# One strip of modulation columns computed behind the last down product of the first feed-forward

## The chip, the cores and the metric

The kernel runs on one core of a Trainium2 chip. The metric is the time of one execution in device microseconds (us). TensorE (PE) multiplies matrices; VectorE (DVE), ScalarE (ACT) and GpSimd (POOL) do the element-wise work; SyncE (SP) issues nearly all loads. Each engine runs its own instructions in order and waits on semaphores for the others. Transfers are issued by SP, ACT and POOL and carried out by the DMA engines.

## The reference

One inference step of a decoder layer for 512 new prompt tokens (one sequence) and 64 sample tokens (eight sequences of eight), 576 token columns in all, with model width 1024. A vector of 9 x 1024 modulation columns per sequence is computed from a conditioning vector by one matrix, and its nine parts shift, scale and gate the three sub-layers:

```
m = jax.nn.silu(c) @ w_ada + b_ada
sh1, sc1, g1, sh2, sc2, g2, sh3, sc3, g3 = jnp.split(m[:, None, :], N_MOD, axis=-1)
h = modulate(rms_norm(x, n1_g), sh1, sc1)
x = x + 0.5 * g1 * swiglu(h, w1_gate, w1_up, w1_down)
h = modulate(rms_norm(x, nm_g), sh2, sc2)
mix, S_new, v_rows = token_mix(h, pos0, S0, w_in, ...)
x = x + g2 * mix
```

A second feed-forward with sh3, sc3, g3 follows. The modulation matrix `w_ada` is 1024 x 9216 in f32, so it is 36 MB of weights that must all be read.

## The kernel before

The kernel keeps the activations transposed, with 128 channels on the partitions and the 576 tokens as columns, and multiplies with f32 weights split into a high and a low part (three matmuls for each product). A weight block is loaded into a raw buffer (`wraw`), ACT casts its high part, DVE subtracts to get the low part, and PE multiplies.

**Strips.** The modulation columns are made in strips of 512 of the 9216 columns. Strips 0 to 3 are made first in another cut. Strips 4 to 17 are made by `ada_strip` (L335): for each half `kk` of the 1024 rows it loads two tiles of 512 KB into the pool `ada` (two buffers), then runs four products with `ada_mm` (L305), each of which fills 32 of the 128 output rows of one PSUM bank. ACT copies the bank (`ada_copy`, L313), PE transposes it in four pieces (`ada_turn`, L319), and `ada_add` sums four groups and adds the bias (DVE, L324 and L328). Strip 10 holds the first half of g2, which is used only after the token mixer.

**Where strips run.** They are generators that `tick` advances by an estimated time, so their instructions fall between the products of the big loops. Strips 4 to 9 run in the first feed-forward. Strips 10 to 17 are started with `start(ada_rest(range(10, 18), 7.0), 9.0)` (L1276) and run in the loop of pairs of w_in columns behind it, called the stream of pairs below (`stream(pair2(w))`).

**Between the two.** The last down product of the first feed-forward is `last_down1`. It has an order written out by hand, `INTO_MIX`; `run` issues the steps in that order and ties each engine except SP to it. The steps named in this text:

- `Dch` is the product for channel block c and token part h; `rsch` adds it to the residual x on DVE (L466); `spch` spills x to DRAM by an ACT-issued transfer (`x1d`, L1223); `sqch`, `adch` form the sum of squares (ACT L428; POOL or DVE L433).
- `rdh`, `rqh`, `qih` turn the sum into 1/rms for half h: a PE product with ones (L444), an ACT reciprocal square root (L448), three DVE steps (L456 to L461). `xph` multiplies x by it (DVE L533); `bpc` and `sp` modulate (ACT L540, DVE L549).
- `N11`, `B21`, `N1`, `B22` and the like, with `h` or `l` and a number, split the modulated blocks into high (ACT L564, L566) and low parts (DVE L571, L575) for PE.
- `h0a0`, `h0a1`, `h0b0` and so on are the products of the first two pairs of w_in columns (L651), and `sn0`, `sn1` copies of their banks (ACT L660). `P1`, `P2`, `P5`, `P6` belong to the third pair.
- `Whc`, `Wlc` split the down weights; those of c = 6 and 7 live in the pool `xs1`, which has three buffers of 9 KB a partition.

SP has no written order; its loads go out in the order in which the scheduler places them, each once its buffer is free.

Of the kernel before, what the change touches and what calls it, by code (L numbers as in the profile page):

```python
# [8 lines left out]
F32 = mybir.dt.float32  # L9
# [6 lines left out]
P = 128  # L16
# [37 lines left out]
INTO_MIX = """  # L54
D00 D01 rs00 Wh2 sp00 sq00 ad00 Wl2 D10 rs01 px0 Wh3 sq01 ad01 Wl3 D11 sp01 rs10 sp10 sq10
ad10 Wh6 D20 rs11 Wl6 px1 sq11 sp11 ad11 D21 Wh4 rs20 sq20 Wl4 sp20 ad20 D30 rs21 Wh5 px2
sq21 Wl5 sp21 ad21 D40 rs30 sq30 sp30 ad30 Wh7 Wl7 D50 rs40 sq40 sp40 nh0 ad40 D60 rs50
sq50 nl0 sp50 ad50 wh0 D70 rs60 sq60 sp60 wl0 ad60 D31 rs70 sq70 nh1 sp70 ad70 nl1 D41 rs31
px3 sq31 sp31 rd0 wh1 D51 ad31 rq0 rs41 px4 q00 sq41 wl1 q10 sp41 ad41 q20 D61 rs51 px5 x00 sq51
sp51 ad51 D71 x10 b000 b010 x20 b100 x30 b110 N11h0 rs71 N11h1 rs61 px7 b210 N11l0 px6  # L60
sq71 N11l1 sq61 sp61 sp71 b300 ad61 h0a0 b310 b200 ad71 B21h3 B21h2 B21l3 B21l2 rd1 sn0 h0a1
rq1 q01 q11 q21 x01 h0b0 x11 b01 b00 s0 b11 s1 b10 tx0 sn1 tx1 N1h0 x21 h0b1 N1h1 N1l0 N1l1
b20 x31 b21 T2a1 b31 b30 h1a0 s3 e0s1 s2 B22h3 N3c1 B22h2 T2b1 N3h1 B22l2 p2bh T2h1 B22l3
h1a1 p2ah p2bl T2l1 e0s0 e0m0 p2al e0m1 N3l1 h1b0 p2S N4c1 p2U N4h1 T2a0 p2Sh P1 e1t0 T2b0
e1m0 p2Sl T2h0 h1b1 e1a0 T2l0 e1s0 P1s p2V N3c0 p2Uh P2 N4c0 N3h0 p2Ul N4h0 P5 e1a1 N3l0
# [19 lines left out]
def layer_kernel(ctx: ExitStack, tc: tile.TileContext, a):  # L85
    nc = tc.nc
    PE, DVE, ACT, POOL = nc.tensor, nc.vector, nc.scalar, nc.gpsimd
# [28 lines left out]
    turn = [0, 0]  # L116
# [17 lines left out]
    def nine(home, shape, dt=F32R):  # L134
        return now[home].tile(shape, dt, tag="x", name=nm(home), bufs=4 if home == "xa" else 3)
# [9 lines left out]
    def bank():  # L145
        return pp.tile([P, 512], F32, tag="ps", name=nm("ps"), bufs=8)
# [51 lines left out]
    def run(order, steps):  # L198

        traced = nc.cur_bb.bb.instructions  # L200
        first = traced[-1]
        for s in order.split():
            steps.pop(s)()
        assert not steps, steps
        at = next(k for k in reversed(range(len(traced))) if traced[k] is first)
        last = {}
        for i in traced[at + 1:]:
            if i.engine != mybir.EngineType.SP:
                if i.engine in last:
# [39 lines left out]
    vec = lines(cst, [P, 104], name="vec")  # L249
# [15 lines left out]
    def ada_tile(shape=(P, 2, 512)):  # L265
        return adas.tile(list(shape), F32, tag="ada", name=nm("ada"), bufs=2)
# [13 lines left out]
    mT = lines(cst, [P, 72, 9], name="mT")  # L280
# [9 lines left out]
    for i in range(2):  # L290
        for n in range(NT):
            rows = P if n < 4 else NS
            t = first.tile([rows, 512], F32, name=nm("xt"))
# [11 lines left out]
    def ada_mm(ps, k, w):  # L305
        g = k % 4
        PE.matmul(
            ps[32 * g:32 * g + 32], lhsT=cs[:, k, :], rhs=w, start=k < 4, stop=k >= 4, tile_position=(0, 32 * g)
        )

    def ada_copy(ps):
        M = now["M"]()
        ACT.copy(out=M, in_=ps)  # L313
        return M

    def ada_turn(M):
        p2 = bank()
        for j in range(4):
            PE.transpose(p2[:, j * P:(j + 1) * P], in_=M[:, j * P:(j + 1) * P], identity=ident)  # L319
        return p2  # L320

    def ada_add(p2, dst, bias):
        t = tp.tile([P, 4, 9], F32, tag="m", name=nm("m"), bufs=2)
        DVE.tensor_reduce(  # L324
            out=t, in_=p2.rearrange("p (j g x) -> p j x g", j=4, g=4)[:, :, 0:9, :],
            axis=mybir.AxisListType.X, op=ALU.add,
        )
        DVE.tensor_tensor(out=dst, in0=t if len(dst.shape) == 3 else t.rearrange("p (m j) c -> p m j c", m=2),  # L328
                          in1=bias, op=ALU.add)
# [25 lines left out]
    class First:  # L355

        def __init__(self, p):
            self.p, self.ws = p, []
            for k in range(KC):
                if k % 4 == 0:  # L360
                    e = nine("xa" if p < 2 or (p, k) == (3, 4) else "xs1", [P, 4, 512], F32)
                w = e[:, k % 4]
                nc.sync.dma_start(
                    out=w.rearrange("p (m c) -> p m c", m=2),
                    in_=a["w_ada"][0, k * P:(k + 1) * P, :].rearrange("p (m c) -> p m c", m=9)[
                        :, 0:2, p * 256:(p + 1) * 256],
                )
# [571 lines left out]
    class Down:  # L939
# [151 lines left out]
    steps = {**operand_steps(Late()), **pair_steps(pairs, greg)}  # L1091
    for c in range(KC):
# [11 lines left out]
        out=xall[:, :, NP:T], in_=psS[:, 0:KC * NS].rearrange("p (c t) -> p c t", c=KC))  # L1104
# [88 lines left out]
    def last_down1(W, product):  # L1193
        finish(rest)
        gate, g, ps, rest_of = gate1m(), a2(), {}, {}
        warm(AF.Abs_reciprocal_sqrt)
        ops.clear()
        ops["near"] = ("B22", "N3", "N4")
        O = Operands(g, 3)
        steps = {}  # L1200
        for c in (2, 3, 6, 4, 5, 7):
            W.load(c)
            steps[f"Wh{c}"] = lambda c=c: W.hi(c)
            steps[f"Wl{c}"] = lambda c=c: W.lo(c)
        w = rg(0), rg(1)
        p = {i: Plain2(w[i][0], i, w[i][1].out, w[i][1].post) for i in range(2)}
        pairs[3] = p[2] = pair2(qk(0))
        steps.update(operand_steps(O))
        ends = pair_steps(p, None)
        for n in ("Gh0", "Gl0", "Gh1", "Gl1"):  # L1210
            ends.pop(n)
        steps.update(ends)
        for c, h in LAST:
            def d(c=c, h=h):
                ps[c, h] = product(c, h)

            def rs(c=c, h=h):
                rest_of[c] = resid(xs[c], ps[c, h], c, h, gate)

            steps[f"D{c}{h}"], steps[f"rs{c}{h}"] = d, rs  # L1220
            steps[f"sq{c}{h}"] = lambda c=c, h=h: n2.square(xs[c], h)
            steps[f"ad{c}{h}"] = lambda h=h: n2.sum(h)
            steps[f"sp{c}{h}"] = lambda c=c, h=h: nc.scalar.dma_start(out=x1d[:, c, HALF[h]], in_=xs[c][:, HALF[h]])  # L1223
            if h:
                steps[f"px{c}"] = lambda c=c: rest_of[c]()
        for h in range(2):
            norm_steps(steps, n2, O, h)

# [44 lines left out]
            yield 6.0  # L1273

    start(operands_of_values(), 4.0)
    start(ada_rest(range(10, 18), 7.0), 9.0)  # L1276
    for w in (
        [qk(hd) for hd in range(1, HEADS)] + [rg(hd) for hd in range(2, HEADS)]
        + [gb(c) for c in range(0, KC, 2)] + [ga(c) for c in range(0, KC, 2)]
# [548 lines left out]
    for pr in ([0], [1], [2], [3], [4], [5], [6, 7]):  # L1828
# [52 lines left out]
    steps = {**operand_steps(O), **pair_steps(pairs, greg)}  # L1881
# [173 lines left out]
```

## Time and profile before

| | before |
|---|---|
| time, median of 3 runs | 1652.28 us (1651.71 to 1655.64) |
| the profiled execution | 1651.52 us |
| its span in the trace | 1649.7 us |
| granted TensorE clock, mean | 0.996 |
| DVE busy | 1152.9 us (70%) |
| ACT busy | 783.2 us (47%) |
| DMA | 252.09 MB, mean 153 GB/s |

The span runs from the first to the last instruction; the profiled execution took 1.82 us more than its span. Busy times are shares of the span. Rows of a timeline give the start in us, the busy time, the engine, the source line, the operation, the tile written and the tiles read, the shapes, the count of merged instructions, and in brackets the idle time of the engine before the row with what ended it.

### The profile page before, as it was taken

Reading aid. Unit: us, or ns where it says so; the run is one execution under the profiler, and the core shown is the slowest. Engines: PE = TensorE matmul, PEld = TensorE weight load, DVE = VectorE, ACT = ScalarE, POOL = GpSimd, SP = SyncE. Lnnn points to the kernel's source line nnn. Section 1 sums busy time; section 2 is a strip of 40 time slices with the busy share of each in tenths; the row PEclk is TensorE's granted clock in tenths of the full one; section 3 lists DMA queues with packets and bytes.
Section 4 is the critical chain, followed back from the end, with each engine's and each line's share of the span. In section 5 each row is a group of like instructions: output and inputs, shape, how many; then the busy total and the mean of one; then the engine's idle time right before and its main releaser. Section 6 shows DMA issues by size and latency. Waiting matters only on the chain. (4 is left out here: it accounts for less than half of the span.)

```text
span 1649.7 us, 31367 instructions
## 1 busy us (share of the span) xinstructions
PE 1618.0 (98%) x12548; PEld 1554.7 (94%) x12548; DVE 1152.9 (70%) x1835; ACT 783.2 (47%) x1331; POOL 292.0 (18%) x372
## 2 busy tenths in 40 slices
PE   7999999999999999999999999999999999999997
PEld 4899999999999999999999999998999999999997
DVE  6867856676697777854788554676848868676773
ACT  5644524344564556553444454443236525343454
POOL 0000000000411111113346343454231000000002
PEclk9999999999999999999999999999999999999999
DMA  9553444332536776765467575799540333332331
GB/s 292 152 157 110 141 129 139 110 110 84 183 115 212 228 214 192 222 196 187 126 192 248 180 172 159 208 261 270 177 141 14 87 93 97 91 96 80 100 90 58
DMA packets 300212, 252.09 MB, mean 153 GB/s; under 512 B 13593, under 2 KB 260633, under 8 KB 300066
## 3 DMA queue, kind: packets, MB, share of 16 engines
q1 hardware_dynamic: 284594, 206.76, 41.5%
q0 software_dynamic: 13168, 40.97, 8.8%
q10 hardware_dynamic: 2304, 2.36, 0.4%
q8 instruction: 98, 1.61, 0.4%
q14 instruction: 48, 0.39, 0.1%
HBM read 207.01 MB, written 43.02 MB: 152 GB/s over the span
## 5 line engine op out<-in xcount | busy, mean ns | idle before, releaser
L651 PE MATMUL ps<-xa,whl 128*128 128x288 f32 x3000 | 420.6, 295 | 5.8 <-ACT xa L564 2.4
L651 PEld LDWEIGHTS ps<-xa,whl 128*128 128x128 f32 x3000 | 401.7, 189 | 18.5 <-issue 5.0
L651 PE MATMUL ps<-xs,whl 128*128 128x288 f32 x2040 | 287.2, 294 | 1.3 <-ACT sn L660 1.1
L651 PEld LDWEIGHTS ps<-xs,whl 128*128 128x128 f32 x2040 | 272.2, 188 | 11.6 <-ACT sn L660 4.6
L679 DVE TENSOR_TENSOR whl<-wraw,whl 128x1024 fp32r<-128x1024 f32 x192 | 234.5, 1223 | 54.0 <-ACT whl L669 45.1
L669 ACT CAST whl<-wraw 128x1024 fp32r<-128x1024 f32 x192 | 200.2, 1048 | 107.0 <-DVE wraw L793 67.3
L485 PEld LDWEIGHTS ps<-c,wd 128*128 128x128 f32 x1824 | 236.7, 188 | 3.5 <-issue 3.4
L485 PE MATMUL ps<-c,wd 128*128 128x320 f32 (+1 forms) x1824 | 239.9, 292 | 0.0
L485 PE MATMUL ps<-c,whl 128*128 128x256 f32 (+1 forms) x1368 | 186.9, 294 | 1.1 <-ACT c L195 0.7
L485 PEld LDWEIGHTS ps<-c,whl 128*128 128x128 f32 x1368 | 179.4, 188 | 3.4 <-ACT c L195 1.2
L472 POOL TENSOR_TENSOR x<-x,s 128x64 f32<-128x64 f32 x72 | 35.2, 489 | 796.9 <-DVE s L471 771.0
L466 DVE SCALAR_TENSOR_TENSOR x<-ps,gate,x 128x320 f32<-128x320 f32 (+1 forms) x128 | 61.1, 481 | 110.7 <-PE ps L485 110.7
L660 ACT COPY sn<-ps 128x288 f32<-128x288 f32 x195 | 77.2, 398 | 104.0 <-PE ps L651 103.7
L188 DVE TENSOR_TENSOR whl<-wraw,whl 128x1024 fp32r<-128x1024 f32 x56 | 76.3, 1364 | 66.7 <-ACT whl L187 66.1
L952 ACT CAST wd<-wraw 128x640 fp32r<-128x640 f32 (+2 forms) x58 | 45.4, 783 | 102.6 <-PE ps L485 95.5
L1353 PE MATMUL ps<-whl,xx 128*128 128x256 f32 x768 | 88.9, 276 | 0.0
L1353 PEld LDWEIGHTS ps<-whl,xx 128*128 128x128 f32 x768 | 88.0, 188 | 0.0
L651 PE MATMUL ps<-xs,whs 128*128 128x288 f32 x480 | 69.1, 292 | 0.0
L187 ACT CAST whl<-wraw 128x1024 fp32r<-128x1024 f32 x56 | 58.6, 1049 | 21.5 <-PE ps L485 13.3
L669 ACT CAST whs<-wraw 128x512 fp32r<-128x512 f32 x62 | 38.4, 620 | 55.7 <-PE ps L651 45.0
L651 PEld LDWEIGHTS ps<-xs,whs 128*128 128x128 f32 x480 | 64.8, 188 | 0.0
L957 DVE TENSOR_TENSOR wd<-wraw,wd 128x640 fp32r<-128x640 f32 (+2 forms) x58 | 53.5, 922 | 10.6 <-ACT wd L952 10.5
(285 smaller groups left out, 2219.0 us busy)
## 6 DMA issues: line engine op xcount, KB each, us to landing
ada<-in_w_ada_dram SPq DMA_DIRECT2D x56, 512.0 KB
wraw<-in_w_in_dram SPq DMA_DIRECT2D x96, 256.0 KB
wraw<-in_w_gate_dram SPq DMA_DIRECT2D x88, 256.0 KB
wraw<-in_w_up_dram SPq DMA_DIRECT2D x88, 256.0 KB
wraw<-in_w_in_dram SPq DMA_DIRECT2D x32, 512.0 KB
wraw<-in_w_down_dram SPq DMA_DIRECT2D x32, 384.0 KB
wraw<-in_w_down_dram SPq DMA_DIRECT2D x32, 320.0 KB
accd<-c POOLq DMA_DIRECT2D x32, 288.0 KB, 5.9
```

The costliest lines, as they stand in the source:

```text
L187: ACT.copy(out=hi, in_=raw)
L188: now["lo"] = (eng or DVE).tensor_tensor(out=lo, in0=raw, in1=hi.bitcast(F32), op=ALU.subtract)
L466: DVE.scalar_tensor_tensor(out=x[:, o:o + w], in0=ps[:, :w], scalar=g[:, c, 0:1], in1=x[:, o:o + w], op0=ALU.mult, op1=ALU.add)
L472: return lambda: POOL.tensor_tensor(out=x[:, NP:T], in0=x[:, NP:T], in1=u, op=ALU.add)
L485: PE.matmul(ps[:, :PW[h]], lhsT=s[:, k, c0:c0 + P], rhs=m[:, PART[h]], start=k == 0 and z == 0, stop=k == kc - 1 and z == 2,)
L651: PE.matmul(ps[:, :H], lhsT=s[:, j * P:(j + 1) * P], rhs=m[:, j, :], start=fresh and j == 0 and z == 0, stop=j == 3 and z == 2, skip_group ...
L660: ACT.copy(out=t, in_=ps[:, :H])
L669: ACT.copy(out=hl[:, 0], in_=src)
L679: now["lo"] = DVE.tensor_tensor(out=hl[:, 1], in0=src, in1=hl[:, 0].bitcast(F32), op=ALU.subtract)
L952: ACT.copy(out=hl[:, 0], in_=self.raw[c])
L957: DVE.tensor_tensor(out=lo, in0=self.raw[c], in1=hi.bitcast(F32), op=ALU.subtract)
L1353: PE.matmul(ps[:, :DV], lhsT=s, rhs=m, start=i == 0, stop=i == 23)
```

## The change

Strip 10 leaves the generators and gets a class `Strip` whose steps stand in `INTO_MIX`:

- Its first two tiles (`load(0)`, in the pool `ada`) are asked for in `last_down1` before the second pair's loads. The other two are halves of one buffer of `xs1` and are asked for by the step `Ad`, behind `Wh7`.
- `A0` and `A1`, eight products in all, stand behind `D71`, the last down product.
- `Ac`, the ACT copy of the bank, stands behind `sn0` and overwrites a part of the first weight tile. `At`, the four transposes, stands behind `rq1`. `Aa`, the reduce and the add on DVE, stands behind `N1l1`.
- The generators start with strip 11.

```diff
-sp51 ad51 D71 x10 b000 b010 x20 b100 x30 b110 N11h0 rs71 N11h1 rs61 px7 b210 N11l0 px6
+sp51 ad51 D71 A0 A1 x10 b000 b010 x20 b100 x30 b110 N11h0 rs71 N11h1 rs61 px7 b210 N11l0 px6
...
+    class Strip:
+        def load(self, kk, w):
+            self.w[kk] = w
+            for i, t in enumerate(w):
+                k0 = 4 * kk + 2 * i
+                nc.sync.dma_start(
+                    out=t,
+                    in_=a["w_ada"][0, k0 * P:(k0 + 2) * P, self.s * 512:(self.s + 1) * 512].rearrange(
+                        "(k p) c -> p k c", p=P),
+                )
+        def mm(self, kk):
+            if kk == 0:
+                self.ps = bank()
+            for g in range(4):
+                ada_mm(self.ps, 4 * kk + g, self.w[kk][g // 2][:, g % 2, :])
+        def copy(self):
+            self.M = self.w[0][0][:, 0]
+            ACT.copy(out=self.M, in_=self.ps)
...
+        strip = Strip(10)
+        strip.load(0, [ada_tile() for _ in range(2)])
...
+        def near():
+            e = nine("xs1", [P, 4, 512], F32)
+            strip.load(1, [e[:, 2 * i:2 * i + 2] for i in range(2)])
+        steps["Ad"], steps["Ac"], steps["At"], steps["Aa"] = near, strip.copy, strip.turn, strip.add
+        for kk in range(2):
+            steps[f"A{kk}"] = lambda kk=kk: strip.mm(kk)
...
-    start(ada_rest(range(10, 18), 7.0), 9.0)
+    start(ada_rest(range(11, 18), 7.0), 9.0)
```

**On PE**, from the end of the last down product (`xw_`, step D71) to the products of the first two pairs. Before:

```order
L485 MATMUL ps_4939<-c_4491,xw_4737 128x256
L651 MATMUL ps_4987<-xa_4965,whl_4763 128x288 x12
L651 MATMUL ps_4988<-xa_4965,whl_4763 128x288 x12
L444 MATMUL ps_5021<-all_4587,onesr 128x288
L651 MATMUL ps_5027<-xa_4965,whl_4840 128x288 x12
L651 MATMUL ps_5028<-xa_4965,whl_4840 128x288 x12
L651 MATMUL ps_4987<-xa_5016,whl_4791 128x288 x12
```

And now, in the changed kernel, where L651 has become L684 and L444 has become L477:

```order
L518 MATMUL ps_4946<-c_4491,xw_4741 128x256
L307 MATMUL ps_4965<-ada_4565,cs 32x512 x2
L307 MATMUL ps_4965<-ada_4566,cs 32x512 x2
L307 MATMUL ps_4965<-xs_635_4743,cs 32x512 x4
L684 MATMUL ps_5003<-xa_4981,whl_4770 128x288 x12
L684 MATMUL ps_5004<-xa_4981,whl_4770 128x288 x12
L477 MATMUL ps_5037<-all_4591,onesr 128x288
L684 MATMUL ps_5044<-xa_4981,whl_4847 128x288 x12
L684 MATMUL ps_5045<-xa_4981,whl_4847 128x288 x12
L319 MATMUL ps_5072<-ident,ada_4565 128x128 x4
L684 MATMUL ps_5003<-xa_5032,whl_4798 128x288 x12
```

Eight products of the strip stand between D71 and h0a0, and four transposes between h0a1 and h0b0; the rest keeps its order.

**On ACT**, from the copies `sn0` (banks of h0a0) to the reciprocal square root of `rq1` (reading `epsT`). Before:

```order
L566 CAST xa_5016<-x_90 128x2x288 x2
L660 COPY sn_5023<-ps_4987 128x288
L660 COPY sn_5025<-ps_4988 128x288
L448 ACTIVATE h_5053<-ps_5021,epsT 128x288
L540 ACTIVATE x_90<-x_90,mT,gain_4543 128x224 x4
```

And on DVE, around the low parts `N1l0`, `N1l1` (reading `tx`). Before:

```order
L533 TENSOR_TENSOR x_90<-x_90,h_5053 128x2x288
L575 TENSOR_TENSOR xa_5102<-tx_5094,xa_5102 128x2x288
L575 TENSOR_TENSOR xa_5102<-tx_5100,xa_5102 128x2x288
L533 TENSOR_TENSOR x_90<-x_90,h_5053 128x2x288
L591 TENSOR_TENSOR x_90<-x_90 128x2x288
```

The same two places now, ACT first:

```order
L599 CAST xa_5032<-x_90 128x2x288 x2
L693 COPY sn_5039<-ps_5003 128x288
L693 COPY sn_5041<-ps_5004 128x288
L415 COPY ada_4565<-ps_4965 128x512
L481 ACTIVATE h_5070<-ps_5037,epsT 128x288
L573 ACTIVATE x_90<-x_90,mT,gain_4543 128x224 x4
```

and DVE:

```order
L566 TENSOR_TENSOR x_90<-x_90,h_5070 128x2x288
L608 TENSOR_TENSOR xa_5124<-tx_5116,xa_5124 128x2x288
L608 TENSOR_TENSOR xa_5124<-tx_5122,xa_5124 128x2x288
L324 TENSOR_REDUCE m_5154<-ps_5072 128x36
L328 TENSOR_TENSOR mT<-m_5154,vec 128x36
L566 TENSOR_TENSOR x_90<-x_90,h_5070 128x2x288
L624 TENSOR_TENSOR x_90<-x_90 128x2x288
```

The copy now stands ahead of `rq1` on ACT, and the reduce and the add ahead of the third and the fourth `x` step of half 1 on DVE.

**On SP**, the loads of the first pairs. In the changed kernel, from the first pair's second raw tile on (before, the row with `xs_635` isn't there and the loads of w_in follow one another; strip 10's first two tiles were already placed far ahead of here and still are):

```order
L719 DMA wraw_4562<-in_w_in_dram 128x4x128 x2
L719 DMA wraw_4569<-in_w_in_dram 128x4x128 x2
L401 DMA xs_635_4743<-in_w_ada_dram 128x2x512 x2
L719 DMA wraw_4572<-in_w_in_dram 128x4x128 x2
L719 DMA wraw_4575<-in_w_in_dram 128x4x128 x2
L719 DMA wraw_4576<-in_w_in_dram 128x4x128 x2
L719 DMA wraw_5430<-in_w_in_dram 128x4x128 x2
L719 DMA wraw_5431<-in_w_in_dram 128x4x128 x2
L343 DMA ada_5556<-in_w_ada_dram 128x2x512
L343 DMA ada_5557<-in_w_ada_dram 128x2x512
L719 DMA wraw_5562<-in_w_in_dram 128x4x128 x2
```

Two transfers of 512 KB now go out ahead of the second half of the second pair's weights, and the first two tiles of strip 11 (the last `ada` rows) go out some loads earlier than strip 10's third and fourth did.

More of the change, by code (lines that the diff above doesn't have):

```diff
@@ L56 @@
 ad10 Wh6 D20 rs11 Wl6 px1 sq11 sp11 ad11 D21 Wh4 rs20 sq20 Wl4 sp20 ad20 D30 rs21 Wh5 px2
-sq21 Wl5 sp21 ad21 D40 rs30 sq30 sp30 ad30 Wh7 Wl7 D50 rs40 sq40 sp40 nh0 ad40 D60 rs50
+sq21 Wl5 sp21 ad21 D40 rs30 sq30 sp30 ad30 Wh7 Ad Wl7 D50 rs40 sq40 sp40 nh0 ad40 D60 rs50
 sq50 nl0 sp50 ad50 wh0 D70 rs60 sq60 sp60 wl0 ad60 D31 rs70 sq70 nh1 sp70 ad70 nl1 D41 rs31
 px3 sq31 sp31 rd0 wh1 D51 ad31 rq0 rs41 px4 q00 sq41 wl1 q10 sp41 ad41 q20 D61 rs51 px5 x00 sq51
-sp51 ad51 D71 x10 b000 b010 x20 b100 x30 b110 N11h0 rs71 N11h1 rs61 px7 b210 N11l0 px6
-sq71 N11l1 sq61 sp61 sp71 b300 ad61 h0a0 b310 b200 ad71 B21h3 B21h2 B21l3 B21l2 rd1 sn0 h0a1
-rq1 q01 q11 q21 x01 h0b0 x11 b01 b00 s0 b11 s1 b10 tx0 sn1 tx1 N1h0 x21 h0b1 N1h1 N1l0 N1l1
+sp51 ad51 D71 A0 A1 x10 b000 b010 x20 b100 x30 b110 N11h0 rs71 N11h1 rs61 px7 b210 N11l0 px6
+sq71 N11l1 sq61 sp61 sp71 b300 ad61 h0a0 b310 b200 ad71 B21h3 B21h2 B21l3 B21l2 rd1 sn0 Ac h0a1
+rq1 At q01 q11 q21 x01 h0b0 x11 b01 b00 s0 b11 s1 b10 tx0 sn1 tx1 N1h0 x21 h0b1 N1h1 N1l0 N1l1 Aa
 b20 x31 b21 T2a1 b31 b30 h1a0 s3 e0s1 s2 B22h3 N3c1 B22h2 T2b1 N3h1 B22l2 p2bh T2h1 B22l3
@@ L390, in add, with __init__, turn @@
             )
+    class Strip:
+        def __init__(self, s):
+            self.s, self.w = s, {}
+        def load(self, kk, w):
[15 more added lines that the diff above has]
+            ACT.copy(out=self.M, in_=self.ps)
+        def turn(self):
+            self.p2 = ada_turn(self.M)
+        def add(self):
+            s = self.s
+            ada_add(self.p2, mT[:, 4 * s:4 * s + 4, :],
+                    vec[:, 4 * s:4 * s + 4].unsqueeze(2).broadcast_to([P, 4, 9]))
     def ada_rest(strips, pause):
@@ L1205, in last_down1 @@
         w = rg(0), rg(1)
-        p = {i: Plain2(w[i][0], i, w[i][1].out, w[i][1].post) for i in range(2)}
+        p = {0: Plain2(w[0][0], 0, w[0][1].out, w[0][1].post)}
+        strip = Strip(10)
+        strip.load(0, [ada_tile() for _ in range(2)])
+        p[1] = Plain2(w[1][0], 1, w[1][1].out, w[1][1].post)
         pairs[3] = p[2] = pair2(qk(0))
```

## The prediction

> **What bounds the kernel now.** I read the page's first part, then who PE waits for, then the timelines of the two places that the change touches.
>
> ```profile
> PE 1618.0 (98%) x12548; PEld 1554.7 (94%) x12548; DVE 1152.9 (70%) x1835; ACT 783.2 (47%) x1331; POOL 292.0 (18%) x372
> 489.00:755.00 266.00, 265.35 (x2030) 248.01 (x2028) 195.02 (x285) 147.46 (x244) 34.05 (x63) 1.00 0.70 217
> ```
>
> PE is busy for 98% of the span, and in the stretch from 489 to 755 us, which holds the stream of pairs with strips 10 to 17, for 265.35 of 266 us. There an instruction taken from PE shortens the kernel by its own time, as long as DVE (195.02 us) and ACT (147.46 us) keep up.
>
> ```profile
> 438.02 4.41 PE L485 MATMUL ps<-c,xw 128*128 128x256 f32 x36
> 444.83 0.40 PE L651 MATMUL ps<-xa,whl 128*128 128x288 f32 x1 [2.40 <-ACT xa L564]
> 445.81 4.78 PE L651 MATMUL ps<-xa,whl 128*128 128x288 f32 x23 [0.58 <-DVE xa L571]
> 450.42 0.65 PE L444 MATMUL ps<-all,onesr 128*128 128x288 f32 x2
> 488.36 2.87 PE L651 MATMUL ps<-xa,whl 128*128 128x288 f32 x20 [0.49 <-DVE whl L679]
> 440.00:445.00 5.00, 2.60 (x22) 2.40 (x20) 5.00 (x11) 3.35 (x7) 2.76 (x4) 1.00 0.52 167
> 445.00:450.00 5.00, 4.42 (x21) 4.21 (x22) 2.92 (x6) 4.63 (x10) 1.73 (x3) 0.66 0.17 59
> ```
>
> Behind D71 PE stands idle from 442.43 to 444.83 us, until ACT has made the first operand of h0a0, and 0.58 us more until DVE has made its low part. This is the place the strip goes to. The row of 445 to 450 shows a second cost: the granted clock falls to 0.66 there. PE next waits at 488.36 us, 0.49 us for weights that DVE splits.
>
> **What leaves the stream.** The removed work is best read where the last strip stands.
>
> ```profile
> 723.31 1.07 PE L307 MATMUL ps<-ada,cs 128*32 128x512 f32 x8
> 724.31 1.84 PE L651 MATMUL ps<-xa,whl 128*128 128x288 f32 x12
> 732.31 1.06 PE L307 MATMUL ps<-ada,cs 128*32 128x512 f32 x8
> 733.31 3.43 PE L651 MATMUL ps<-xs,whl 128*128 128x288 f32 x24
> 736.58 0.60 PE L319 MATMUL ps<-ident,ada 128*128 128x128 f32 x4
> 736.93 0.48 PE L1353 MATMUL ps<-whl,xx 128*128 128x256 f32 x2
> ```
>
> From the start of one row to the next, a half strip holds PE for 1.00 us (twice) and the transposes for 0.35 us, so one strip costs 2.35 us. The seven strips that are left keep their places one slot earlier, and the stream loses **2.35 us** of PE time. Nothing is late in its stead: DVE and ACT are less than three quarters busy there, and their copy, reduce and add of this strip leave too.
>
> **What it costs at the new place.** A0 and A1 take 2 x 1.00 us behind D71, so they end at 444.43, 0.40 us before the operand that ends the wait (444.83). They are free as long as their weights are there. The first two tiles were placed by SP far ahead already; the other two get their issue slot behind the first pairs' loads.
>
> ```profile
> 417.38 22.84 SPq L686 DMA_DIRECT2D wraw<-in_w_in_dram  x16
> 422.00:426.00 4.00, 4.00 (x30) 4.00 (x29) 1.42 (x2) 1.93 (x4) 1.76 (x3) 1.00 0.94 285
> 426.00:430.00 4.00, 4.00 (x30) 4.00 (x29) 2.73 (x4) 2.59 (x4) 1.81 (x2) 1.00 0.84 252
> 434.00:438.00 4.00, 4.00 (x34) 3.89 (x34) 2.21 (x6) 2.21 (x4) 1.41 (x3) 1.00 0.51 148
> 432.18 0.45 ACT L428 ACTIVATE h<-x 128x288 f32<-128x288 f32 x1 [2.13 <-DMA x1d<-x]
> 435.72 0.44 ACT L428 ACTIVATE h<-x 128x288 f32<-128x288 f32 x1 [2.15 <-POOL x L472]
> ```
>
> Sixteen loads of w_in go out in 22.84 us from 417.38; the two new ones stand seventh and eighth, so at an even pace of 1.4 us they leave at about 426 to 427 us (an estimate). Their 1.05 MB last 3.7 to 4.2 us at the 285 and 252 GB/s that this stretch moves, and land some 10 us before A1. The loads behind them come that much later: the second pair's second half and the third pair's. SP's queue behind them is not held up otherwise, since the buffer in `xs1` was last read by the previous pair's products. ACT issues the spills of x, and such an issue can wait for an earlier transfer; ACT has idle times of 2.13 and 2.15 us just there, and the transfers have room again from 434 on (148 GB/s). I cost this at nothing; the bounds are nothing and a late `rq0`, priced below as a rival.
>
> Strip 11's first two loads now go out behind At, past which SP next issues at 475.25:
>
> ```profile
> 475.25 3.36 SPq L686 DMA_DIRECT2D wraw<-in_w_in_dram  x4
> ```
>
> At is done by about 455, so they hold up nobody.
>
> **The path that ends at 488.36.** The freed time is only kept up to the next wait, so I follow what feeds it.
>
> ```profile
> 446.83 1.66 ACT L540 ACTIVATE x<-x,mT,gain 128x288 f32<-128x288 f32 x3 [0.29 <-issue]
> 448.41 1.23 ACT L566 CAST xa<-x 128x576 fp32r<-128x576 f32 x2
> 449.54 0.39 ACT L660 COPY sn<-ps 128x288 f32<-128x288 f32 x1
> 450.62 0.40 ACT L660 COPY sn<-ps 128x288 f32<-128x288 f32 x1 [0.70 <-PE ps L651]
> 451.11 0.50 ACT L448 ACTIVATE h<-ps,epsT 128x288 f32<-128x288 f32 x1
> 451.65 0.46 DVE L456 SCALAR_TENSOR_TENSOR h<-h 128x288 f32<-128x288 f32 x1 [1.12 <-ACT h L448]
> 458.87 0.75 DVE L533 TENSOR_TENSOR x<-x,h 128x576 f32<-128x576 f32 x1
> 459.66 1.04 ACT L540 ACTIVATE x<-x,mT,gain 128x224 f32<-128x224 f32 x2 [0.96 <-DVE x L533]
> 463.59 0.76 DVE L575 TENSOR_TENSOR xs<-x,xs 128x576 fp32r<-128x576 f32 x1 [0.90 <-ACT xs L566]
> 465.00:470.00 5.00, 5.00 (x40) 5.00 (x40) 4.97 (x8) 2.08 (x5) 0.00 (x0) 1.00 0.00 0
> 475.00:480.00 5.00, 5.00 (x41) 5.00 (x40) 5.00 (x9) 4.56 (x8) 0.60 (x2) 1.00 0.76 218
> L313 ACT COPY ada<-ps x18: 567/587/599, 23.7 to 733.7; 128x512 f32<-128x512 f32 x18
> L324 DVE TENSOR_REDUCE m<-ps x18: 296/303/310, 26.3 to 737.2; 128x36 f32<-128x144 f32 x18
> L328 DVE TENSOR_TENSOR mT<-m,vec x18: 184/196/198, 26.6 to 737.6; 128x36 f32<-128x36 f32 x18
> ```
>
> It runs from `rq1` on ACT (451.11) to DVE without a break until 458.87, from there through ACT (459.66) back to DVE at 463.59, and then DVE is busy without rest (4.97 and 5.00 of 5 us) until it delivers the weights of 488.36. Whatever stands in this chain delays PE there, however early PE comes.
>
> The full clock moves its start. A full-clock run of 24 such matmuls starts 3.12 us before its successor:
>
> ```profile
> 466.52 3.28 PE L651 MATMUL ps<-xs,whl 128*128 128x288 f32 x24
> 469.64 1.72 PE L651 MATMUL ps<-xa,whl 128*128 128x288 f32 x12
> ```
>
> That is 0.130 us each; the 23 of h0a0 take 4.61 us (445.81 to 450.42) where 2.99 would do. If A0 and A1 keep the clock up, h0a0 ends 1.62 us earlier, at 448.80. But ACT is busy until 449.54 anyway: the first copy stays there, the second and Ac follow it at once, and `rq1` can start at 449.54 + 0.39 + 0.40 + 0.59 = 450.92, or at 450.65 where back-to-back rows start 0.09 us before the last one ends. Of 1.62 us only 0.19 to 0.46 reaches `rq1`; I take 0.3. Aa adds 0.30 + 0.20 = 0.50 us to DVE ahead of the step at 458.87. The chain ends **0.2 us later** (0.04 to 0.31). The transposes (0.35 us) and the rest of PE's gain end in longer waits between 480 and 488, so they count neither way.
>
> **Sum**: -2.35 + 0.2 = -2.15 us. On the profiled execution of 1651.52 us this gives 1649.4. That execution lies 0.76 us under the median of 1652.28, so the forecast for a median is **1650.1 us**.
>
> **The clock, weighed against the skill.** The row of 445 to 450 shows a half clock behind idle times of 2.40 and 0.58 us. The Trainium skill ("TensorE: Matmul & The Clock Gate", "What's actually happening") has the clock fall only after a whole idle window of about 3.4 us. By that rule there would be nothing to win at h0a0, and the sum would be the -1.35 us of rival 2; the trace does not agree, since one matmul stood inside the idle time and the clock fell all the same.
>
> **Rivals.**
>
> 1. *The clock's gain is kept whole.* If the chain to 488.36 has slack that the rows don't show, PE keeps -2.35 - 1.62 + 0.35 = -3.62 us: 1648.7. For it speaks the 1.12 us for which DVE waited on `rq1`; against it the DVE rows without idle time. 17%.
>
> 2. *The clock falls all the same*, or falls at another place. Then h0a0 ends at 450.42 as before, Ac runs from 451.02 to 451.61 ahead of `rq1` (+0.50), Aa adds 0.50, and the net is -1.35: 1650.9. A second such stretch stands later in the trace:
>
> ```profile
> 1289.83 0.80 PE L651 MATMUL ps<-xa,whl 128*128 128x288 f32 x4 [1.38 <-ACT whl L669]
> 1291.46 4.43 PE L651 MATMUL ps<-xa,whl 128*128 128x288 f32 x20 [0.83 <-DVE whl L679]
> ```
>
> There 20 matmuls took 4.43 us in place of 2.6, so the same event at a new place costs up to 1.8 us and brings the sum to -2.15 + 1.8 = -0.35: 1651.9; the one at 1291 may also vanish, for -1.8. 18%.
>
> 3. *Slower.* The 1.05 MB push the weight loads behind them, ACT waits at the spill issues and at the second pair's cast, and `rq0`, the x steps and h0a0 start late. It decides where the delay exceeds ACT's 2.15 us of idle time plus the 2.35 us won. At the 148 GB/s of the row of 434 to 438 the transfer would take 7.1 us, so 7.1 - 2.15 = 4.9 us late at 444.83 and 2.6 us slower in all: 1654.9. Against it: that row's rate is low for want of work, as its DMA share of 0.51 says. 7%.
>
> 4. *The change does not do what it says*: A1's weights arrive later than 442.43, and PE waits for them rather than for ACT, giving the 2.35 us back, about 1652. About 15 us lie between issue and use. 3%.
>
> **How the numbers follow.** The forecast holds 55%. The range reaches from 1647.0, rival 1 with the event at 1291 gone for most of it, to 1653.0, which takes in rivals 2 and 4 and the spread of the runs before, and leaves out the slow end. A difference of 0.3% is 5.0 us, about what a measurement of this kernel can tell from no change. Every case but the outermost lies inside it: faster by more needs rival 1 and a second event gone (1648.7 - 1.8 = 1646.9), for which I give 10%; slower by more needs twice the price of rival 3, 3%; within it 87%.
>
> **What would show it.** In the profile of the changed kernel: eight L307 matmul pairs directly behind the last `xw` row and PE idle there for under 0.6 us before h0a0; a clock of 1.00 in the 5 us behind it; `rq1` within 0.5 us of its old distance from D71's end; longer PE waits for DVE between 480 and 490; and from there to the first scores of the mixer 2.3 us less than before. It is wrong if PE waits behind D71 for a transfer, if ACT idles before the second pair's cast, or if the waits near 488 are no longer than before.

## The result, and the profile after

| | before | after |
|---|---|---|
| median of the runs timed together | 1651.71 us (11 runs, 1649.84 to 1655.64) | 1647.91 us (11 runs, 1646.13 to 1650.25) |
| the profiled execution | 1651.52 us | 1647.73 us |
| its span | 1649.7 us | 1646.0 us |
| granted TensorE clock, mean | 0.996 | 0.995 |

The changed kernel takes 0.9978 of the time before, 95% interval 0.9970 to 0.9986, which is 3.6 us less (2.3 to 5.0). A second timing in other runs gave the same ratio, 0.9978 (0.9969 to 0.9987). The forecast was 2.15 us less. One execution of the kernel with transposes in the gap (below) took 4101.63 us and is left out of that kernel's ratio. The mean clock of the profiled execution did not rise, because this one ran at half clock from 28.44 to 35.26 us, far ahead of the places of the change. The page's line of busy times of the changed kernel shows PE's 2.9 us lower (1618.0 before); the span less the busy time, PE's idle time, fell by 0.8 us:

```profile
PE 1615.1 (98%) x12548; PEld 1553.8 (94%) x12548; DVE 1153.0 (70%) x1835; ACT 782.1 (48%) x1331; POOL 293.7 (18%) x372
```

**The new place.** PE's timeline of the changed kernel behind D71, where L518, L684 and L477 are the former L485, L651 and L444, and then at the waits for split weights:

```profile
437.24 4.41 PE L518 MATMUL ps<-c,xw 128*128 128x256 f32 x36
441.58 1.06 PE L307 MATMUL ps<-ada,cs 128*32 128x512 f32 x8
442.47 1.04 PE L307 MATMUL ps<-xs,cs 128*32 128x512 f32 x8
444.06 0.40 PE L684 MATMUL ps<-xa,whl 128*128 128x288 f32 x1 [0.55 <-ACT xa L597]
445.06 3.29 PE L684 MATMUL ps<-xa,whl 128*128 128x288 f32 x23 [0.59 <-DVE xa L604]
448.19 0.65 PE L477 MATMUL ps<-all,onesr 128*128 128x288 f32 x2
...
481.60 1.59 PE L684 MATMUL ps<-xa,whl 128*128 128x288 f32 x10 [0.27 <-DVE whl L712]
...
487.45 2.88 PE L684 MATMUL ps<-xa,whl 128*128 128x288 f32 x20 [0.46 <-DVE whl L712]
```

Both half strips run without a wait, and h0a0 starts 6.82 us behind the start of D71's last row, as before (444.83 - 438.02 = 6.81). The windows of the same place (busy us of each engine, then the granted clock, the DMA share and GB/s) show that the half clock is gone:

```profile
440.00:445.00 5.00, 3.91 (x32) 2.05 (x30) 5.00 (x10) 4.13 (x8) 3.14 (x5) 1.00 0.71 199
445.00:450.00 5.00, 4.94 (x36) 4.84 (x37) 2.68 (x4) 4.58 (x12) 1.12 (x2) 1.00 0.31 116
```

h0a0 is 448.19 - 444.06 = 4.13 us long instead of 5.59. ACT and DVE in the changed kernel (L415 is Ac, L481 `rq1`, L324 and L328 Aa, L566 the step at 458.87 of before):

```profile
448.91 0.68 ACT L693 COPY sn<-ps 128x288 f32<-128x288 f32 x2
449.49 0.58 ACT L415 COPY ada<-ps 128x512 f32<-128x512 f32 x1
449.97 0.51 ACT L481 ACTIVATE h<-ps,epsT 128x288 f32<-128x288 f32 x1
```

```profile
457.73 0.30 DVE L324 TENSOR_REDUCE m<-ps 128x36 f32<-128x144 f32 x1
458.06 0.20 DVE L328 TENSOR_TENSOR mT<-m,vec 128x36 f32<-128x36 f32 x1
458.18 0.75 DVE L566 TENSOR_TENSOR x<-x,h 128x576 f32<-128x576 f32 x1
```

Counted from the start of h0a0, `rq1` comes at 449.97 - 444.06 = 5.91 us (6.28 before), the DVE step at 14.12 us (14.04 before) and PE's restart of 487.45 at 43.39 us (43.53 before). h0a0 is 1.46 us shorter. The strip's four transposes take 0.43 us of that (by the pairing of matmuls described below), and the chain through ACT, DVE and the split weights hands back all but 0.14 us of the rest.

**The stream.** PE's timeline where strip 17 stood, in the kernel before:

```profile
720.10 3.28 PE L651 MATMUL ps<-xs,whl 128*128 128x288 f32 x24
...
725.98 1.72 PE L651 MATMUL ps<-xa,whs 128*128 128x288 f32 x12
```

and the same rows of the changed kernel, with nothing between:

```profile
718.63 3.28 PE L684 MATMUL ps<-xs,whl 128*128 128x288 f32 x24
721.75 1.72 PE L684 MATMUL ps<-xa,whl 128*128 128x288 f32 x12
723.31 1.72 PE L684 MATMUL ps<-xa,whs 128*128 128x288 f32 x12
```

From the 24 matmuls to the row `whs` it is 5.88 us before and 4.68 after. A half strip therefore costs 1.20 us, not 1.00: the row ahead of it lasts 0.09 us longer (723.31 - 720.10 = 3.21 against 3.12) and the row behind it 0.11 us longer (725.98 - 724.31 = 1.67 against 1.56).

**Two smaller places.** In both kernels the half strip at 698 us (strip 16's before, strip 17's now) takes longer than the usual 1.07 us, because the weight loads of its last four products wait for the strip's transfer (0.87 us before, 0.22 us after). First before, with that wait, then after:

```profile
698.83 2.07 PE L307 MATMUL ps<-ada,cs 128*32 128x512 f32 x8
699.84 0.14 PEld L307 LDWEIGHTS ps<-ada,cs 128*32 128x32 f32 x4 [0.87 <-DMA ada<-in_w_ada_dram]
```

```profile
698.01 1.42 PE L307 MATMUL ps<-ada,cs 128*32 128x512 f32 x8
```

And the first scores of the mixer wait longer for POOL. Before, then after:

```profile
755.48 1.16 PE L1383 MATMUL ps<-c,c 128*128 128x128 f32 x8 [1.13 <-POOL c L1331]
```

```profile
751.70 1.16 PE L1426 MATMUL ps<-c,c 128*128 128x128 f32 x8 [1.71 <-POOL c L1374]
```

### The profile page after: what moved, and what is told of

It is laid out like the page before. It is cut to its first block, busy times and chain, and to the rows that moved or that the text cites. A ratio compares the mean times of both kernels' runs of the same rounds, so it can differ in the third digit from the quotient of the medians.

```text
span 1646.0 us, 31371 instructions
## 1 busy us (share of the span) xinstructions
PE 1615.1 (98%) x12548; PEld 1553.8 (94%) x12548; DVE 1153.0 (70%) x1835; ACT 782.1 (48%) x1331; POOL 293.7 (18%) x372
## 4 chain that ended last, share of the span: by engine, by line
PE 80%; DVE 8%; DMA 4%; ACT 3%; issue 3%; POOL 1%; SPq 1%; ACTq 0%; POOLq 0%; DVEq 0%
PE ps L684 36%; PE ps L518 29%; PE ps L1396 4%; PE ps L1626 3%; PE ps L307 2%; DVE whl L712 1%; DMA wraw<-in_w_down_dram 1%; ACT whl L702 1%; PE ps L1526 1%; DMA xa<-in_w_ada_dram 1%; PE ps L1488 1%; PE ps L1532 1%; PE ps L1409 1%; DMA rope<-in_rope_dram 1%; DMA wraw<-in_w_in_dram 0%
## 5 line engine op out<-in xcount | busy, mean ns | idle before, releaser
L684 PE MATMUL ps<-xa,whl 128*128 128x288 f32 x3000 | 419.4, 294 | 4.2 <-DVE whl L712 1.6
L684 PEld LDWEIGHTS ps<-xa,whl 128*128 128x128 f32 x3000 | 400.2, 188 | 17.1 <-issue 3.4
L684 PE MATMUL ps<-xs,whl 128*128 128x288 f32 x2040 | 287.1, 294 | 1.6 <-ACT sn L693 1.6
L684 PEld LDWEIGHTS ps<-xs,whl 128*128 128x128 f32 x2040 | 272.1, 188 | 11.3 <-issue 5.0
L518 PEld LDWEIGHTS ps<-c,wd 128*128 128x128 f32 x1824 | 236.7, 188 | 3.5 <-issue 3.4
L518 PE MATMUL ps<-c,wd 128*128 128x320 f32 (+1 forms) x1824 | 239.9, 292 | 0.0
L518 PE MATMUL ps<-c,whl 128*128 128x256 f32 (+1 forms) x1368 | 186.9, 294 | 1.1 <-ACT c L195 0.6
L518 PEld LDWEIGHTS ps<-c,whl 128*128 128x128 f32 x1368 | 179.5, 188 | 3.3 <-DVE c L196 0.9
L684 PE MATMUL ps<-xs,whs 128*128 128x288 f32 x480 | 69.1, 292 | 0.0
L684 PEld LDWEIGHTS ps<-xs,whs 128*128 128x128 f32 x480 | 64.8, 188 | 0.0
```

Source lines behind the costliest of these rows:

```text
L518: PE.matmul(ps[:, :PW[h]], lhsT=s[:, k, c0:c0 + P], rhs=m[:, PART[h]], start=k == 0 and z == 0, stop=k == kc - 1 and z == 2,)
L684: PE.matmul(ps[:, :H], lhsT=s[:, j * P:(j + 1) * P], rhs=m[:, j, :], start=fresh and j == 0 and z == 0, stop=j == 3 and z == 2, skip_group ...
```

## The experiments

To compare two traces I paired their PE matmuls in order, those of strips left out, and took how much later each one starts (negative: earlier). The table gives what such a pairing with the first profile of before gains or loses between two places: from h0a0's start to the restart at 488, from there to 698, to 706 (the late half strip), to 754 (the place of the last strip), at the first scores, and from there to 1280. At h0a0's start the profiles stand -1.7 to +1.1 us from the first one of before, most of it from the first 125 us, and the repeat of before stands 1.24 us from its own first: that part is chance.

| kernel | 445 to 488 | to 698 | to 706 | to 754 | scores | to 1280 |
|---|---|---|---|---|---|---|
| before, repeated | +1.63 | +0.40 | +0.32 | -0.02 | +0.17 | +0.01 |
| after | -0.14 | +0.09 | -0.65 | -2.89 | +0.57 | -0.01 |
| after, second | -0.25 | +0.39 | -0.94 | -2.88 | +0.63 | -0.28 |
| after, third | -0.19 | +0.31 | -0.52 | -2.84 | +0.24 | -0.27 |
| strip left out | -0.05 | +0.40 | +0.13 | -2.88 | +0.17 | -0.32 |
| transposes in the gap | -1.22 | +0.02 | -0.35 | -0.03 | +1.33 | +1.53 |
| strip in the busy stretch | +2.72 | +0.11 | -0.27 | -2.88 | +0.89 | +1.60 |
| no Ac, At, Aa | -1.20 | +0.11 | -0.88 | -2.89 | +0.09 | -0.06 |
| Ac, At, Aa late | -0.98 | +0.08 | -0.69 | -2.88 | +0.55 | -0.21 |
| the same, second | -0.97 | +0.15 | -0.14 | -2.88 | -0.10 | -0.07 |
| first place empty | -0.25 | -2.50 | +0.10 | +0.00 | +0.03 | +0.05 |

**Both kernels profiled again.** No edit.

> The kernel before, profiled a second time. If the differences that I put down to chance are chance, its PE matmuls stand against the first profile of before by some tenths of a microsecond up to D71 (the first pair of profiles showed -0.78 us there between before and after), and the 2.07 us of the half strip at 698.83 us and the 1.13 us wait for POOL at 755 us come out otherwise. If these belong to the program, they come again: 2.0 to 2.1 us and 1.1 us.

> The changed kernel, profiled a second time. What the change does should come again: no half clock at h0a0, PE waits for split weights at 481 to 488 us of 0.3 to 0.5 us each, 2.3 (my forecast's strip) or 2.9 us (the first pair of profiles) won where the removed strip stood, and a wait for POOL at 751.7 of 1.7 us. The -0.78 us up to D71 should change if it is chance.

The strip's 2.9 us and the waits near 488 came again in the changed kernel. The late weights and the wait for POOL did not repeat in size: at 698 to 706 the three profiles of after gain 0.5 to 0.9 us, the scores lose 0.2 to 0.6. What I had not expected stands in the repeat of before. Its timeline of h0a0 and its windows:

```profile
444.58 5.89 PE L651 MATMUL ps<-xa,whl 128*128 128x288 f32 x23 [0.58 <-DVE xa L571]
```

```profile
445.00:450.00 5.00, 5.00 (x22) 5.00 (x22) 2.20 (x4) 3.39 (x7) 0.93 (x1) 0.50 0.17 59
450.00:455.00 5.00, 5.00 (x35) 4.80 (x35) 3.12 (x7) 1.89 (x5) 0.57 (x1) 0.92 0.07 29
```

The half clock lasted twice as long (the last section shows why), h0a0's 23 matmuls took 5.69 us instead of 4.61, `rq1` came 7.61 us behind h0a0's start instead of 6.28, and at the restart PE was 1.63 us later. So the kernel before pays a price at this place that differs from execution to execution, and the gain of the change there runs from 0.2 us against one profile to 1.9 us against the other.

**The strip left out.**

```diff
-    start(ada_rest(range(10, 18), 7.0), 9.0)
+    start(ada_rest(range(11, 18), 7.0), 9.0)
...
+    POOL.memset(mT[:, 40:44], 0.0)
```

> Strip 10 is left out altogether (the first half of the columns of g2 is zero). The idle time and the half clock at 445 us stay. Theory A (the strip costs PE 2.9 us in the stream, chain unchanged): -2.9 us in the stream against before, -2.3 with 0.57 lost again at the wait for POOL. Theory B (2.35 us as forecast, the rest of the first comparison chance): -2.35 at most, -1.8 with the wait for POOL. Rival: if the clock's gain at 445 us was what made the changed kernel faster, leaving the strip out gives 1 us less than the change did.

The ratio to before is 0.9987 (0.9978 to 0.9996), 2.1 us less. Up to 488 nothing changes (-0.05; h0a0 is 5.54 us long), and the stream loses 2.88 us: theory A's price. The rival came true as well: without the strip at the new place the gain is 1.5 us smaller than that of the change, so filling the gap seems to be worth something beyond hiding the strip, though the two intervals overlap.

**The gap filled, the strip not moved.**

```diff
-sp51 ad51 D71 x10 ...
+sp51 ad51 D71 Z x10 ...
...
+        def warm_up():
+            z = bank()
+            for _ in range(22):
+                PE.transpose(z[:, 0:P], in_=ident, identity=ident)
```

> The kernel before with 22 PE transposes behind D71, into a bank that nothing reads; no strip moves. The clock should stay at 1.00 at 445 us and h0a0 end some 1.6 us earlier. Theory A (a chain on ACT and DVE ends at the wait of 488 us whatever PE does): the gain is given back between 480 and 490 us, 0 to -0.4 us in all. Theory B (PE's gain is kept): -1.6 us. If the transposes don't count for the clock, the half clock stays and the time is unchanged.

PE's timeline:

```profile
440.62 2.56 PE L1237 MATMUL ps<-ident 128*128 128x128 f32 x22
443.19 0.40 PE L651 MATMUL ps<-xa,whl 128*128 128x288 f32 x1
444.16 3.28 PE L651 MATMUL ps<-xa,whl 128*128 128x288 f32 x23 [0.58 <-DVE xa L571]
447.27 0.65 PE L444 MATMUL ps<-all,onesr 128*128 128x288 f32 x2
...
753.58 1.77 PE L1389 MATMUL ps<-c,c 128*128 128x128 f32 x8 [2.46 <-POOL c L1337]
```

The clock stayed full and h0a0 shrank to 4.08 us. Theory A, that PE's gain is handed back by a chain that ends when it ends, falls: 1.22 us were still there at 488. The chain itself starts with h0a0, since `rq1` needs the product with ones behind it, and it started 0.99 us earlier (`rq1` 5.29 us behind h0a0's start instead of 6.28). Of theory B's 1.6 us, three quarters were kept there. The time did not show it: the ratio is 1.0003 (0.9992 to 1.0014). Where the other executions lose the gain is not shown. In the profiled one it went at the first scores, where PE waited 2.46 us for POOL and the clock fell behind that (0.77 in the window), +1.33 and +1.53 us.:

```profile
755.00:760.00 5.00, 5.00 (x35) 4.66 (x35) 2.81 (x6) 1.56 (x3) 2.87 (x3) 0.77 0.36 110
```

**The strip where PE has work.**

```diff
-sp51 ad51 D71 A0 A1 x10 ...
+sp51 ad51 D71 x10 ...
...
-... sn0 Ac h0a1 rq1 At q01 q11 q21 x01 h0b0 x11 b01 b00 s0 b11 s1 b10 tx0 sn1 tx1 N1h0 x21 h0b1 ...
+... sn0 h0a1 rq1 q01 q11 q21 x01 h0b0 A0 A1 x11 b01 b00 s0 b11 s1 b10 tx0 sn1 Ac tx1 N1h0 x21 At h0b1 ...
```

> The changed kernel with A0 and A1 not in the gap behind D71 but behind h0b0, where PE has work, and Ac and At behind them. Theory A (the strip is free only because the gap was idle): the gap of 2.4 + 0.6 us and the half clock at 445 us come back, the strip costs PE about 2.4 to 2.9 us between 450 and 480 us, of which PE's wait of 0.5 us at 488 us covers a part: about 2.4 us later at 490 us than the kernel before (from the same D71), 2.9 us won in the stream as in the changed kernel, so within 1 us of before in all, and 2.5 to 3 us slower than the changed kernel. Theory B (the place is indifferent; the gain is all made in the stream): as the changed kernel, -3.5 us against before.

PE's timeline has the idle times and the slow h0a0 again, and a wait of the transposes for the copy (L415):

```profile
445.95 0.40 PE L684 MATMUL ps<-xa,whl 128*128 128x288 f32 x1 [2.40 <-ACT xa L597]
446.93 4.84 PE L684 MATMUL ps<-xa,whl 128*128 128x288 f32 x23 [0.58 <-DVE xa L604]
...
458.43 1.06 PE L307 MATMUL ps<-ada,cs 128*32 128x512 f32 x8
459.31 1.04 PE L307 MATMUL ps<-xs,cs 128*32 128x512 f32 x8
461.06 0.66 PE L319 MATMUL ps<-ident,ada 128*128 128x128 f32 x4 [0.71 <-ACT ada L415]
```

At the restart it stands 2.72 us later than before, and the stream gives back 2.88: theory A. Taken with the smaller places, the strip moved without the gap is worth 0.3 us in the trace up to 754. The ratio is 0.9992 (0.9983 to 1.0000), 2.3 us behind the change by the ratios.

**Without Ac, At and Aa**, with A0 and A1 left in the gap, and strip 10's columns zero.

```diff
-... sn0 Ac h0a1 rq1 At q01 ... N1l0 N1l1 Aa
+... sn0 h0a1 rq1 q01 ... N1l0 N1l1
```

> The changed kernel with A0 and A1 in the gap, but without Ac, At and Aa: strip 10's columns (the first half of g2) are zero. It shows what these three cost at the new place. Theory A: rq1 0.5 to 0.6 us earlier, DVE 0.5 us more, PE 0.35 to 0.5 us more: -1.0 us at 490 us and in all against the changed kernel, the same as the kernel that moves them behind the chain. Theory B (hidden): no change at 490 us.

`rq1` comes 5.31 us behind h0a0's start, 0.6 earlier than in the changed kernel, and the restart 1.0 us earlier (-1.20 against -0.14 to -0.25): theory A. The ratio, 0.9969 (0.9959 to 0.9978), is 1.5 us below the change's, with intervals that overlap.

**Ac, At and Aa behind the chain.** The same result as the change, with these three moved.

```diff
-... sn0 Ac h0a1 rq1 At q01 q11 q21 x01 h0b0 x11 ... N1l0 N1l1 Aa
+... sn0 h0a1 rq1 Ac q01 q11 q21 x01 h0b0 At x11 ... N1l0 N1l1
...
+    def late_add():
+        t = tp.tile([P, 4, 9], F32, tag="m", name=nm("m"), bufs=2)
+        in_order([now["lo"], DVE.tensor_reduce(out=t, ...)])
+        DVE.tensor_tensor(out=mT[:, 40:44, :], in0=t, ...)
+        yield 0.0
+    start(late_add(), 3.5)
```

> The changed kernel with Ac moved behind rq1 on ACT, At behind h0b0 on PE, and the reduce and add of Aa pushed out on DVE to behind the splits that PE waits for at 488 us. Theory A (the chain through rq1 and DVE sets PE's restart at 481 to 488 us; Ac costs it 0.5 to 0.6 us and Aa 0.5 us): rq1 starts 12.1 us behind the start of D71's last row instead of 12.7, and PE's waits for split weights at 481 and 488 us come 0.9 to 1.1 us earlier; 0.9 to 1.1 us faster than the changed kernel. Theory B (PE or a load ends last there, Ac and Aa are hidden): no change against the changed kernel.

ACT, DVE and PE in the first of its two profiles (L1288 and L1292 are Aa):

```profile
448.96 0.69 ACT L693 COPY sn<-ps 128x288 f32<-128x288 f32 x2
449.54 0.50 ACT L481 ACTIVATE h<-ps,epsT 128x288 f32<-128x288 f32 x1
449.93 0.58 ACT L415 COPY ada<-ps 128x512 f32<-128x512 f32 x1
```

```profile
485.42 2.36 DVE L712 TENSOR_TENSOR whl<-wraw,whl 128x1024 fp32r<-128x1024 f32 x2
487.70 0.30 DVE L1288 TENSOR_REDUCE m<-ps 128x36 f32<-128x144 f32 x1
487.91 1.21 DVE L712 TENSOR_TENSOR whl<-wraw,whl 128x1024 fp32r<-128x1024 f32 x1
489.05 0.18 DVE L1292 TENSOR_TENSOR mT<-m,vec 128x36 f32<-128x36 f32 x1
```

```profile
486.69 2.87 PE L684 MATMUL ps<-xa,whl 128*128 128x288 f32 x20 [0.46 <-DVE whl L712]
```

`rq1` starts 449.54 - 444.15 = 5.39 us behind h0a0's start and the restart comes 0.8 us earlier than in the changed kernel (-0.98 and -0.97 against -0.14 to -0.25), near the 0.9 to 1.1 expected. Whether the time keeps it was asked with a second timing, beside the changed kernel:

> The changed kernel once more, timed beside the version with Ac, At and Aa moved behind the chain (the next run). By the four profiles without another loss: waits for split weights at 481 to 488 us, a POOL wait of 1.7 us, a half clock at 1288 us in some executions.

> The version with Ac behind rq1, At behind h0b0 and Aa behind the splits of 488 us, once more. Theory A (the chain): 0.9 us earlier at 490 us than the changed kernel, and a median 0.5 to 1.2 us lower, as the first 11 runs (0.7 us) and the kernel without Ac, At and Aa (1.1 us) showed. Theory B (the 0.9 us are taken back by a longer wait or a half clock behind 750 us): medians equal within 0.3 us.

The ratios to before are 0.9977 (0.9968 to 0.9986) and 0.9964 (0.9952 to 0.9977), the changed kernel's 0.9978 both times. Over all its executions the version has a median of 1646.72 us (17, 1643.82 to 1651.39), the changed kernel one of 1648.17 us (23, 1646.13 to 1651.07). The trace shows theory A's 0.8 us at 488, kept up to 1280; the medians point the same way, but with intervals that overlap they do not prove it. In the second timing alone, the version's six executions have a median of 1644.89 us against 1648.17, 3.3 us lower where 0.5 to 1.2 was expected, and that is more than the chain gives: neither of its profiles has the half clock near 1288 us that all three of the change have (last section), and that fall costs 1.4 to 1.6 us. A straight line through all 17 and all 23 executions, with the granted clock of each as a second term, puts the version 0.7 us below the change at equal clock (give or take 0.8), and the kernel without Ac, At and Aa 1.0 us (give or take 0.7), as the traces do.

**The first place of the stream empty instead of the last.**

```diff
-    start(ada_rest(range(11, 18), 7.0), 9.0)
+    start(ada_rest(range(11, 18), 7.0), 36.0)
```

> The changed kernel with strips 11 to 17 started 27 us of planned time later, so that they stand where they stand in the kernel before, and the first strip's place in the stream is empty instead of the last one's. Theory A: the four matmuls (0.11 us each) that moved ahead of the last pair's last row stand behind it again, so PE's wait for POOL at 752 us is 1.1 to 1.3 us as before instead of 1.7, -0.5 us; but the late weights of strip 16's second half at 699 us (1.0 to 1.3 us too long in two profiles of before, 0 to 0.35 in two of after) come back with the old places, +0.6 to +1.3 us. In all 0 to +0.8 us against the changed kernel. Theory B (both are chance): no difference but that of two profiles, and the stream's 2.9 us come out at the strip that is missing.

PE's timeline at the late half strip and at the scores:

```profile
696.13 2.11 PE L307 MATMUL ps<-ada,cs 128*32 128x512 f32 x8
...
752.92 1.16 PE L1426 MATMUL ps<-c,c 128*128 128x128 f32 x8 [1.16 <-POOL c L1374]
```

The strip's price moves to the stream's first place (-2.50 with +0.3 of another late half strip in it), the late half strip is as long as before, and the scores wait 1.16 us: theory A in this profile. The ratio, 0.9981 (0.9972 to 0.9990), cannot be told from the change's. The other profiles weaken both parts: with the strips one place earlier the half strip at 698 us holds PE for 1.00 to 2.07 us, in the old places for 1.64 to 2.27; and the wait for POOL is 1.03 to 2.02 us in the kernels with the order of the change and 1.13 to 2.46 in those with the order of before. Both have a tendency and a scatter as large as it.

## Why the prediction was right in kind and short in size

**The strip's price was undersized.** The step "one strip costs 2.35 us" took the distance from the strip's row to the next. Left out were 0.09 us that the row ahead takes longer and 0.11 us that the row behind takes longer, at each half, and about 0.13 at the transposes. Eight profiles of the five kernels without the last strip gain 2.84 to 2.89 us at that place. This is the surest part of the result, 0.5 us more than forecast.

**The places A0 and A1 are free**, as forecast: h0a0 starts 6.82 us behind D71's last row as before, so rival 3 (late loads) and rival 4 (late weights for A1) did not occur. Put where PE has work, the same strip costs as much as the stream wins.

**The clock behaved as forecast, the chain nearly.** h0a0 became 1.46 us shorter (forecast 1.62). `rq1` with Ac ahead of it came 0.37 us earlier (forecast 0.3, bounds 0.19 to 0.46). The step behind Aa came 0.08 us later in one profile and 0.04 earlier in the second, and the restart 0.14 to 0.25 us earlier in three, where "the chain ends 0.2 us later" was the forecast: a miss of 0.4 us. The reading of the chain was too stiff in one point. It does not end "however early PE comes": with nothing added to it, it gives 1.2 of the 1.5 us on (the kernels with transposes in the gap and without Ac, At, Aa). In the change Ac (0.5 to 0.6 us ahead of `rq1`) and Aa (0.5 us on DVE) use these up. Rival 1 is therefore half right: the clock's gain is real and kept, and spent on the added work. That its sum of -3.62 us comes close to the measured -3.6 is luck: of the clock's 1.62 us less 0.35 for the transposes, 0.14 to 0.25 were left against the first profile of before, and the stream gave 2.88 instead of 2.35.

**The signs named in advance** came as written, but for one size: PE is idle for 0.55 us behind the strip, the clock there is 1.00, `rq1` comes 8.32 us behind D71's end (8.68 before), the waits for split weights are 0.27 and 0.46 us instead of 0.49 in all, and from the restart to the first scores the changed kernel gains 2.88 us instead of 2.3. The prediction took 5.0 us as about the least that a measurement can tell from no change; eleven runs of each kernel told 3.6 us, with an interval of 2.3 to 5.0.

**What the forecast did not know** is that the price of the half clock varies in the kernel before. It was sized from one profile, where h0a0's 23 matmuls lose 1.6 us. In the repeat they lost 2.7 and all of it reached 488 (2.85 us lie there between it and the kernel with the transposes in the gap). The change is worth 0.2 us at this place against the one and 1.9 us against the other. That the change, at -3.6 us, is ahead of the strip left out, at -2.1, fits this, but with the overlap of the intervals it is an inference.

**Not in the forecast**: 0.5 to 0.9 us less waiting in the half strip at 698, and 0.2 to 0.6 us more at the scores. The first comparison's sum, taken from the profile, is -0.78 (start, chance) - 0.14 + 0.09 - 0.65 - 2.89 + 0.57 = -3.80, against a span 3.7 us shorter. Of it the -2.89 is the change's for certain; the -0.14 holds against this profile of before alone, and the -0.65 and the +0.57 are within the scatter of these two places.

**Still open**: why the half strip at 698 waits for its weights, and what sets the wait for POOL at the scores, which follows a wait of DVE for transfers of the mixer's inputs (4.99 us before, 5.34 after, 6.29 with the transposes in the gap). No run changed either alone.

## What to carry to other kernels

Work put into an idle gap of PE has two effects that the gap does not show: its copies and adds lengthen the chain that the next wait hangs on (1.0 us here, most of which could be moved behind the chain), and PE's clock may stay up because the gap is gone. Half clocks elsewhere come and go from execution to execution, so small differences are better compared between executions with the same granted clock. The price of a short block among long rows is read from the row ahead of it to the second row behind it, in two traces or two places, not from its own start to the next.

## What the runs showed of the hardware that was not expected

**Short idle times halve the clock where enough of them fall into one stretch of a raster.** Behind D71, with 2.40 and 0.58 us idle and one matmul between, the clock fell in all four profiles of kernels that leave the gap, and in none of the eight that fill it. Near 1288 us PE idles 1.38 and 0.83 us with four matmuls between; there the clock fell in seven of twelve profiles, with the same idle times. The row of 20 matmuls behind them in the changed kernel and in the repeat of before:

```profile
1287.67 4.44 PE L684 MATMUL ps<-xa,whl 128*128 128x288 f32 x20 [0.83 <-DVE whl L712]
```

```profile
1292.76 2.88 PE L651 MATMUL ps<-xa,whl 128*128 128x288 f32 x20 [0.84 <-DVE whl L679]
```

It costs 1.4 to 1.6 us each time (the loss or gain between 1280 and 1300 in the pairing). At the scores the clock fell behind waits of 2.02 and 2.46 us and behind none of the ten of 1.03 to 1.76 us.

What decides can be read from the times at which the traces record a change of the granted clock. Within each trace they all lie whole multiples of 3.413 us apart, and this raster stands elsewhere in each execution, 0.12 to 3.00 us behind the first instruction. Here are windows cut along it near 1288 us, before and then its repeat (the first number is the window's length, the next PE's busy time):

```profile
1288.81:1292.22 3.41, 1.55 (x9) 1.33 (x10) 3.41 (x5) 3.41 (x4) 0.00 (x0) 1.00 0.00 0
1292.22:1295.64 3.42, 3.42 (x17) 3.42 (x16) 3.35 (x5) 0.44 (x2) 0.00 (x0) 0.50 0.81 233
```

```profile
1287.04:1290.45 3.41, 2.71 (x21) 2.48 (x19) 3.26 (x8) 1.42 (x3) 0.00 (x0) 1.00 0.00 0
1290.45:1293.87 3.42, 1.90 (x12) 1.68 (x13) 3.42 (x5) 3.10 (x4) 0.00 (x0) 1.00 0.01 3
```

In the first, most of the two idle times lies in one stretch, PE is idle for 1.86 of its 3.41 us, and the next stretch runs at half clock. In the repeat a border cuts the first idle time in two, no stretch has more than 1.52 us idle, and the clock stays up. From 20 us to the end of all twelve traces, with the clock full, it fell behind each of the 25 stretches with 1.95 us idle or more, behind 6 of the 15 with 1.65 to 1.94 us, and behind none of the over 5000 with less. Ahead of the program's end the half clock lasted one stretch, and two in the three cases where PE idled 0.58 us or more in the first of them. One of these is h0a0 in the repeat of before:

```profile
443.95:447.36 3.41, 2.83 (x12) 2.78 (x12) 1.82 (x3) 3.11 (x8) 1.68 (x2) 0.50 0.24 87
447.36:450.77 3.41, 3.41 (x15) 3.27 (x15) 1.43 (x2) 1.59 (x4) 0.00 (x0) 0.50 0.00 0
```

The Trainium skill ("TensorE: Matmul & The Clock Gate", "What's actually happening") describes windows of about 3.4 us that run freely, so that the same program meets them at another phase each time. The raster of 3.41 us and the scatter at 1288 agree with that. That a whole idle window is needed does not: 1.65 us were enough.

These events, at up to three places of one execution, are as large as most of what this study measures, and can explain a good part of the spread of 4 to 8 us among the executions of one kernel: of the changed kernel's, the three with a mean clock of 0.998 average 1646.36 us and the six with 0.995 1648.72 us, and of the version with Ac, At and Aa late, the five with 0.998 average 1644.62 us and the three with 0.995 1649.91 us.
